# Where tiles lie in on-chip memory: a hybrid attention block with its working tiles placed anew

## The chip, the cores and the metric

The kernel runs on one core of a Trainium2 chip. The core has a matrix engine (TensorE, PE in the profile, with its weight load as PEld), a vector engine (VectorE, DVE), a scalar engine (ScalarE, ACT), GpSimd (POOL), and SyncE (SP), whose queue issues the DMAs. All of them work on one memory of 128 partitions; a tile takes the same stretch of bytes in each partition, so its address is an offset into the partition. The metric is the device time of one execution in microseconds; of several runs the median counts.

## The reference

One layer of a hybrid encoder on x of 1024 tokens by 1024 channels, float32:

```python
h = rms_norm(x, g_pre)
u = einsum('bsd,dn->bsn', h, w_in)            # 10 parts of 512 columns and 3 x 1024 merge gates
y_pool = pool_mixer(pool_v, pool_w, pool_scale) * silu(pool_g)
y_conv = conv_mixer(conv_x, conv_gb, conv_gc, conv_w, conv_b) * silu(conv_g)
y_sb   = stick_breaking_attention(sb_q, sb_k, sb_v) * silu(sb_g)
proj   = einsum('bsnw,nwd->bsnd', stack([y_pool, y_conv, y_sb], 2), w_branch)
merged = sum(sigmoid(merge) * proj, axis=2)
out    = einsum('bsd,de->bse', merged, w_out)
return x + rms_norm(out, g_post)
```

## The kernel before

Every float32 operand of a large product is split into a rounded high part and the remaining low part (`split`, L72: ACT casts the high part at L73, DVE or POOL subtracts at L74). A product of two operands then is three matmuls: high by high, high by low, low by high. TensorE works with a stationary operand of 128 columns and a moving operand of up to 512 columns; a `128x512` matmul is the unit in nearly all that follows. PE works off its instructions in the order of the program, and so does every other engine.

The stages, with their times in the profiled execution:

- **0 to 34 us**: x is normed and transposed into the tiles `hh` and `hl` (high and low part of h).
- **34 to 338 us**: attention, with the input projections that it needs in its gaps (`half_block`, L189), and then two products of the scheme below.
- **338 to 383 us**: the attention branch's projection (`branch_proj`, L491): 8 blocks of 24 matmuls, whose moving operands are the y tiles `yhi`, `ylo`. Beside it DVE and ACT form sums of quarters of h, `t1`, `t2`, `t3` (`build_quarters`, each with a high and a low tile); a fourth, t4, overwrites b12 in `hh`, `hl`.
- **383 to 919 us**: 24 pairs of input-projection blocks (4 for the pool branch, 8 for the conv branch, 12 for the merge gates). Each pair takes seven quarter products instead of eight (`run_pair`, L564; `product`, L530), each of 12 matmuls, in the order b11, t2, b21, t3, t1, t4, b22. So 36 of a pair's 84 matmuls read a `t1`, `t2` or `t3` tile, and 48 read `hh` and `hl`. The small matmuls `mx` of the pool branch (L648, 24 in all) and the projections of the pool and conv branches (L491) lie between pairs.
- **919 to 968 us**: the last four conv projections. For each half of a block, DVE multiplies the projection by the gate (L716), POOL adds the partial sum (L717), ACT casts the merged result's high part `m` and DVE subtracts its low part (L73, L74, called from `take_merged`, L732). In the same stretch the weights of the output projection are split (`oh`, `wo`).
- **968 to 1048 us**: the output projection (`out_products`, L791): its stationary operands are the `m` tiles, its moving ones `oh` and `wo`.

Weights come in by DMA (`w_raw`, `s_raw`), are cast by ACT and subtracted by POOL, two weights ahead of the product that reads them; three buffers each hold the high and the low parts (`wsp`). What fixes an address are the pools: they are stacked in the order in which they are opened, from the lower end upward, or with `side="right"` from the upper end downward. A pool with `reuse_waits="tile"` may take the place of tiles whose last use is still to come; its first write then waits for that use.

The merged result for channels 0 to 511 (d below 4) is finished early, kept in device memory (`proj_d`), and fetched again near the end, in `taken_back`:

```python
m = held["m"].tile([P, S], F32, tag="mr", name="mr", bufs=2)
nc.sync.dma_start(m, proj_d[d])
take_merged(d, slice(0, S), m)
```

The first of these steps is called ahead of the four last projections, and one more step with each half of a projection (`take`, L762). `mr` and the four `m` tiles lie in a pool `fin` that is opened where `t1`, `t2` and `t3` were.

## Time and profile before

| | us |
|---|---|
| median of 3 runs (1045.95 to 1049.87) | 1049.41 |
| the profiled execution | 1049.73 |
| its span, first to last instruction | 1048.0 |
| PE busy | 1004.6 (96%) |
| DVE, POOL, ACT busy | 625.9, 460.1, 449.4 |
| mean granted TensorE clock | 0.988 |

About 1.7 us of the profiled execution lie outside its span. PE is busy nearly throughout; consecutive matmuls overlap (the one begins while the other drains), so the cost of a matmul in a full stretch is the time from its start to the next one's start, which is less than the duration that the profile gives for one. The chain of waits that ended last shows it: a piece `x192` of 44.88 us holds 192 matmuls, one every 44.88 / 192 us.

### The profile page before, as it was taken

To read this page: it belongs to the slowest core of one execution; us is meant where nothing else is said; L and a number is where in the kernel's file an instruction comes from. 1 tells how busy PE (TensorE), PEld (TensorE's weight loads), DVE (VectorE), ACT (ScalarE), POOL (GpSimd) and SP (SyncE) were. 2 spreads that over 40 slices of the span, in tenths; PEclk is the share of its full clock that TensorE was granted. 3 is DMA by queue.
4 is the path that set the end of the run, shared out by engine and by line. 5 is a ranking of instruction groups with operands and counts; after the bars stand their busy time and mean duration, and the time that the engine had idled before them with its cause. 6 is when DMAs were issued, how large, how long until landed. Compare 5 with 4: busy or idle time off the path is not lost.

```text
span 1048.0 us, 13308 instructions
## 1 busy us (share of the span) xinstructions
PE 1004.6 (96%) x4752; PEld 829.0 (79%) x4752; DVE 625.9 (60%) x847; ACT 449.4 (43%) x879; POOL 460.1 (44%) x367
## 2 busy tenths in 40 slices
PE   4999999999998999999999999998999999998997
PEld 3788878888887888888888888886888888876886
DVE  6556777667777968798677675554333543342133
ACT  6567667567755543332222234333233332443111
POOL 3043544535472024455454444444555555576000
PEclk9999999999999999999999999998999999999999
DMA  6101000101011532122122134545333454164033
GB/s 229 53 21 41 22 21 21 41 21 32 21 31 41 191 131 71 61 70 91 61 81 61 61 111 144 190 136 173 118 120 124 161 171 131 34 221 157 1 121 121
DMA packets 45138, 97.09 MB, mean 93 GB/s; under 512 B 5392, under 2 KB 5648, under 8 KB 45072
## 3 DMA queue, kind: packets, MB, share of 16 engines
q1 hardware_dynamic: 44928, 95.71, 28.0%
q8 instruction: 38, 0.62, 0.2%
q10 hardware_dynamic: 144, 0.52, 0.1%
q14 instruction: 28, 0.23, 0.1%
HBM read 73.15 MB, written 23.07 MB: 92 GB/s over the span
## 4 chain that ended last, share of the span: by engine, by line
PE 82%; ACT 5%; DVE 4%; POOL 4%; issue 3%; DMA 2%; POOLq 0%; SPq 0%; DVEq 0%; ACTq 0%
PE g_ps L539 26%; PE q_ps L539 17%; PE g_ps L189 12%; PE pp L491 10%; PE o_ps L796 7%; PE o L418 3%; PE tp L404 2%; DVE sn L386 2%; PE z L382 1%; PE z L379 1%; ACT sn L383 1%; POOL sp L388 1%; POOL g L717 1%; DMA pr<-yp 1%; DMA xt<-in_x_dram 1%
## 5 line engine op out<-in xcount | busy, mean ns | idle before, releaser
L74 POOL TENSOR_TENSOR w_lo<-s,w_hi 128x512 fp32r<-128x512 f32 x95 | 130.7, 1376 | 173.8 <-ACT w_hi L73 171.2
L74 POOL TENSOR_TENSOR w_lo<-s_raw,w_hi 128x512 fp32r<-128x512 f32 x70 | 94.6, 1351 | 102.6 <-ACT w_hi L73 96.8
L388 POOL TENSOR_TENSOR sp<-sp,sn 128x127 f32<-128x127 f32 (+3 forms) x64 | 81.2, 1272 | 132.8 <-DVE sn L386 69.0
L386 DVE TENSOR_TENSOR_SCAN sn<-sn,zeros 128x128 f32<-128x128 f32 (+3 forms) x64 | 100.6, 1574 | 48.2 <-ACT sn L383 45.5
L73 ACT CAST w_hi<-s 128x512 fp32r<-128x512 f32 x96 | 59.6, 621 | 134.1 <-PE g_ps L539 65.7
L73 ACT CAST w_hi<-s_raw 128x512 fp32r<-128x512 f32 x70 | 43.5, 621 | 138.2 <-PE g_ps L539 53.8
L189 PE MATMUL g_ps<-hh,w_hi 128*128 128x512 f32 x240 | 99.4, 414 | 0.3 <-ACT hh L285 0.3
L189 PE MATMUL g_ps<-hl,w_hi 128*128 128x512 f32 x240 | 94.5, 394 | 0.3 <-DVE hl L286 0.3
L189 PE MATMUL g_ps<-hh,w_lo 128*128 128x512 f32 x240 | 94.5, 394 | 0.0
L74 POOL TENSOR_TENSOR w_lo<-w_raw,w_hi 128x512 fp32r<-128x512 f32 x44 | 68.2, 1550 | 56.3 <-ACT w_hi L73 56.3
L539 PE MATMUL g_ps<-hh,w_hi 128*128 128x512 f32 x236 | 92.6, 392 | 0.0
L539 PE MATMUL g_ps<-hh,w_lo 128*128 128x512 f32 x236 | 92.1, 390 | 0.0
L539 PE MATMUL g_ps<-hl,w_hi 128*128 128x512 f32 x236 | 91.8, 389 | 0.0
L491 PE MATMUL pp<-yhi,w_lo 128*128 128x512 f32 x192 | 77.1, 402 | 5.0 <-ACT yhi L73 2.6
L491 PE MATMUL pp<-ylo,w_hi 128*128 128x512 f32 x192 | 76.8, 401 | 0.9 <-DVE ylo L74 0.9
L491 PE MATMUL pp<-yhi,w_hi 128*128 128x512 f32 x192 | 76.4, 399 | 0.0
L383 ACT ACTIVATE sn<-z 128x384 f32<-128x384 f32 (+2 forms) x96 | 47.9, 499 | 29.7 <-PE z L382 20.3
L232 DVE TENSOR_TENSOR wl<-tp,wh 128x512 fp32r<-128x512 f32 (+2 forms) x96 | 50.4, 545 | 15.4 <-ACT wh L405 14.9
L539 PE MATMUL q_ps<-hh,w_hi 128*128 128x512 f32 x148 | 58.1, 392 | 0.0
L539 PE MATMUL q_ps<-hh,w_lo 128*128 128x512 f32 x148 | 57.8, 391 | 0.0
L539 PE MATMUL q_ps<-hl,w_hi 128*128 128x512 f32 x148 | 57.5, 389 | 0.0
L405 ACT CAST wh<-tp 128x512 fp32r<-128x512 f32 (+2 forms) x96 | 44.6, 493 | 21.8 <-PE tp L404 17.2
(204 smaller groups left out, 2426.4 us busy)
## 6 DMA issues: line engine op xcount, KB each, us to landing
s_raw<-in_w_in_dram SPq DMA_DIRECT2D x96, 256.0 KB, 2.6
pr<-proj SPq DMA_DIRECT2D x48, 256.0 KB, 3.3
proj<-g SPq DMA_DIRECT2D x20, 512.0 KB, 2.9
w_raw<-in_w_in_dram SPq DMA_DIRECT2D x34, 256.0 KB, 2.6
w_raw<-in_w_branch_dram SPq DMA_DIRECT2D x24, 256.0 KB, 2.6
xt<-in_x_dram SPq DMA_DIRECT2D x8, 512.0 KB, 7.9
proj<-proj SPq DMA_DIRECT2D x8, 512.0 KB, 2.7
wo_raw<-in_w_out_dram SPq DMA_DIRECT2D x16, 256.0 KB, 2.9
```

The source lines that it names most:

```text
L73: nc.scalar.copy(hi, raw)
L74: eng.tensor_tensor(out=lo, in0=raw, in1=f32(hi), op=ALU.subtract)
L189: nc.tensor.matmul(ps, l[:, a], r[k // 4][t][:, k % 4, :], start=(n == 0), stop=(n == 3 * KB - 1))
L232: nc.vector.tensor_tensor(out=o, in0=a, in1=f32(b), op=ALU.subtract)
L383: nc.scalar.activation(sn[:, c0:c1], z[:, :w], AF.Sigmoid, scale=-0.125)
L386: nc.vector.tensor_tensor_scan(out=rev, data0=rev, data1=zeros.to_broadcast([P, n]), initial=1.0, op0=ALU.mult, op1=ALU.max)
L388: nc.gpsimd.tensor_tensor(out=sp[:, 0:n - 1], in0=sp[:, 0:n - 1], in1=sn[:, 1:n], op=ALU.mult)
L405: nc.scalar.copy(wh[c][:, 0:m, qsub], tp[:, 0:m, :])
L418: nc.tensor.matmul(o[:, cs], vc[:, j, s, :], wt[j // 4][:, j % 4, cs], start=(j == 0 and wt is wl), stop=(j == i and wt is wh))
L491: nc.tensor.matmul(pp, l[:, a], r[:, HALVES[t]], start=(n == 0), stop=(n == 3 * NB - 1))
L539: nc.tensor.matmul(bank, l[:, a], r[:, j, :], start=(n == 0), stop=(n == 11))
L796: nc.tensor.matmul(ps, l[:, a], r[:, es], start=(d == 0 and n == 0), stop=(d == KB - 1 and n == 2))
```

## The change

The calculation and PE's order of instructions stay as they are. The pools `wraw`, `ysb`, `sraw`, `ssum`, `gates` and `tmps` move to the upper end; `quarters`, `stp` and `ysp` move to the lower side. The pool of the quarter sums is never closed: the `m` tiles of d below 4, a tile `back` in place of the two `mr`, and a tile `late` for the post-norm gain are further tiles of it.

```diff
-    wraw = op("wraw", 3)
+    wraw = op("wraw", 3, side="right")
-    ysb_pool = ysb_stack.enter_context(tc.tile_pool(name="ysb", bufs=4))
+    ysb_pool = ysb_stack.enter_context(tc.tile_pool(name="ysb", bufs=4, side="right"))
...
-    tpool, close_t = pool_of("quarters", 6, side="right")
+    tpool = op("quarters", 6, reuse_waits="tile")
...
-    stp, close_stp = pool_of("stp", 2, side="right")
-    ysp, close_ysp = pool_of("ysp", 4, side="right")
+    ysp, close_ysp = pool_of("ysp", 4)
+    stp, close_stp = pool_of("stp", 2)
...
-    held["raw"] = op("sraw", 5, reuse_waits="tile")
-    held["sum"] = op("ssum", 3, reuse_waits="tile")
+    held["raw"] = op("sraw", 5, side="right", reuse_waits="tile")
+    held["sum"] = op("ssum", 3, side="right", reuse_waits="tile")
...
-    tmps, close_tmps = pool_of("tmps", 1, side="right")
+    gpool = op("gates", 4, side="right", reuse_waits="tile")
+    tmps = op("tmps", 1, side="right", reuse_waits="tile")
...
-    gpool = op("gates", 4, reuse_waits="tile")
...
-            o = (held["m"].tile([P, 2, S], F32R, tag="m", name="m", bufs=4) if d < 4
-                 else bigp.tile([P, 2, S], F32R, tag="big", name="m"))
+            o = tpool.tile([P, 2, S], F32R, tag="t", name="m") if d < 4 else bigp.tile([P, 2, S], F32R, tag="big", name="m")
...
+        back = tpool.tile([P, 2, S], F32, tag="t", name="back")
...
-                m = held["m"].tile([P, S], F32, tag="mr", name="mr", bufs=2)
+                m = back[:, d % 2, :]
...
-    close_tmps()
-    close_t()
-    held["m"] = op("fin", 1, side="right", reuse_waits="tile")
...
-    fin = held["m"]
-    gpost_sb = fin.tile([P, D], F32, tag="gpost", name="gpost_sb")
+    fin = op("fin", 1, reuse_waits="tile")
+    late = tpool.tile([P, 2, S], F32, tag="t", name="late")
+    gpost_sb, junk = late[:, 0, :], late[:, 1, 0:HALF]
```

The addresses that follow from it, in KiB from the start of a partition, with the remainder of the start address by 64 bytes (all are multiples of 32):

| tiles | read by TensorE | before, KiB | rest | after, KiB | rest |
|---|---|---|---|---|---|
| `w_hi`, `w_lo` | yes | 24 to 36 | 0 | 18 to 30 | 0 |
| `hh`, `hl`; `m` of d from 4, `oh` | yes | 36 to 100 | 0 | 30 to 94 | 0 |
| `t1`, `t2`, `t3` | yes | 176 to 224 | 32 | 94 to 142 | 0 |
| y of the attention branch | yes | 124 to 156 | 32 | 142 to 174 | 0 |
| y of the pool and conv branches, `wo` | yes | 136 to 168 | 0 | 142 to 174 | 0 |
| `ph`, `pl` (read by `mx`) | yes | 124 to 132 | 0 | 190 to 198 | 32 |
| `m` of d below 4 | yes | 185 to 217 | 32 | 102 to 118, 126 to 142 | 0 |
| `mr`; after `back` | no | 177 to 185 | 32 | 118 to 126 | 0 |
| `w_raw`, `s_raw`, `s` | no | 18 to 24, 100 to 116 | 0 | 202 to 224 | 32 |
| gates, `pr` | no | 116 to 136 | 0 | 182 to 202 | 32 |
| `m1`, `u2`, `u3` | no | 170 to 176 | 32 | 176 to 182 | 32 |

All operands that TensorE reads in the attention stage start at a rest of 0 before and after.

The new places let some instructions be written earlier. On ACT, around the last pair of merge gates, the order before is this (`g_8288` and `g_8289` are the last pair's gates, `w_hi_...` its weights and the next projection's, `m_8439` and `m_8474` the high parts of d = 0 and 1):

```order
L73 CAST w_hi_8350<-s_raw_8242 128x512
L594 ACTIVATE g_8288<-g_8288 128x512
L73 CAST w_hi_8370<-s_8368 128x512
L73 CAST w_hi_8392<-w_raw_8390 128x512
L594 ACTIVATE g_8289<-g_8289 128x512
L73 CAST w_hi_8413<-w_raw_8411 128x512
L73 CAST m_8439<-mr_8437 128x1024
L594 ACTIVATE g_8289<-g_8289 128x512
L73 CAST m_8474<-mr_8472 128x1024
L73 CAST w_hi_8453<-w_raw_8451 128x512
L594 ACTIVATE g_8288<-g_8288 128x512
```

The same place of ACT after, where the `m` tiles of d = 0 to 3 are 8434, 8468, 8494 and 8530:

```order
L73 CAST w_hi_8350<-s_raw_8242 128x512
L73 CAST m_8434<-back_8432 128x1024
L595 ACTIVATE g_8288<-g_8288 128x512
L73 CAST w_hi_8370<-s_8368 128x512
L73 CAST m_8468<-back_8432 128x1024
L73 CAST w_hi_8392<-w_raw_8390 128x512
L73 CAST m_8494<-back_8432 128x1024
L595 ACTIVATE g_8289<-g_8289 128x512
L73 CAST w_hi_8413<-w_raw_8411 128x512
L73 CAST m_8530<-back_8432 128x1024
L595 ACTIVATE g_8289<-g_8289 128x512
```

All four casts now stand among the last pair's weight casts; before, two stood behind them and the other two among the projections. The first `back` transfer waits for the last product that reads `t2` (its place in memory); the transfers into the same half of `back` (d = 2 after 0, 3 after 1) wait for DVE's subtraction of the earlier one.

On DVE before, from the last pair into the last projections (`g_8136` and `g_8137` are gates of the pair before, `pp` a projection's result, `m_8496` and `m_8560` the merged blocks of d = 4 and 5):

```order
L585 TENSOR_TENSOR g_8289<-g_ps_8396,u3_8292 128x512
L74 TENSOR_TENSOR m_8439<-mr_8437,m_8439 128x1024
L585 TENSOR_TENSOR g_8288<-g_ps_8417,u2_8291 128x512
L74 TENSOR_TENSOR m_8474<-mr_8472,m_8474 128x1024
L716 TENSOR_TENSOR g_8136<-pp_8457,g_8136 128x512
L74 TENSOR_TENSOR m_8496<-g_8136,m_8496 128x512
L716 TENSOR_TENSOR g_8136<-pp_8481,g_8136 128x512
L74 TENSOR_TENSOR m_8501<-mr_8499,m_8501 128x1024
L74 TENSOR_TENSOR m_8538<-mr_8536,m_8538 128x1024
L716 TENSOR_TENSOR g_8137<-pp_8519,g_8137 128x512
```

The same stretch of DVE after (there `m_8490` and `m_8552` are the blocks of d = 4 and 5):

```order
L74 TENSOR_TENSOR m_8434<-back_8432,m_8434 128x1024
L586 TENSOR_TENSOR u3_8292<-q_ps_8354,u2_8291 128x512
L74 TENSOR_TENSOR m_8468<-back_8432,m_8468 128x1024
L586 TENSOR_TENSOR u2_8291<-g_ps_8374,u2_8291 128x512
L586 TENSOR_TENSOR g_8289<-g_ps_8374,u3_8292 128x512
L74 TENSOR_TENSOR m_8494<-back_8432,m_8494 128x1024
L586 TENSOR_TENSOR g_8289<-g_ps_8396,u3_8292 128x512
L74 TENSOR_TENSOR m_8530<-back_8432,m_8530 128x1024
L586 TENSOR_TENSOR g_8288<-g_ps_8417,u2_8291 128x512
L715 TENSOR_TENSOR g_8136<-pp_8452,g_8136 128x512
L74 TENSOR_TENSOR m_8490<-g_8136,m_8490 128x512
L715 TENSOR_TENSOR g_8136<-pp_8475,g_8136 128x512
```

The subtractions for d = 2 and 3, which stood between two multiplications of the last projections, now stand among the last pair's sums. At the start of the pool branch (383 us) a few casts and memsets change places as well.

## Rows read from the trace of the kernel before

**Rows 1.** Stretches: start:end, length, busy (count) by engine, PEclk, DMA share, GB/s.
```profile
338.00:383.00 45.00, 45.00 (x195) 35.94 (x194) 38.40 (x61) 22.71 (x41) 1.29 (x1) 1.00 0.49 169
701.00:720.00 19.00, 15.50 (x61) 11.24 (x60) 10.12 (x14) 8.94 (x16) 6.61 (x5) 0.90 0.47 150
912.00:968.00 56.00, 48.94 (x205) 39.16 (x204) 20.46 (x29) 23.06 (x39) 38.85 (x28) 0.95 0.57 188
```

**Rows 2.** Chain that ended last: start us, us, what, count.
```profile
337.79 44.88 PE pp L491 x192
...
749.06 10.88 PE pp L491 x48
...
967.66 73.90 PE o_ps L796 x334
```

**Rows 3.** Stretch of five pairs, line L539 alone: PE and PEld busy (count), clock, DMA.
```profile
562.47:659.27 96.80, 96.80 (x421) 78.81 (x421) 1.00 0.33 108
```

**Rows 4.** PE's groups by shape, whole span: out<-in, count, busy us, mean ns.
```profile
L539 PE MATMUL g_ps<-hh,w_hi 128*128 128x512 f32 x236 | 92.6, 392 | 0.0
...
L539 PE MATMUL g_ps<-hl,w_hi 128*128 128x512 f32 x236 | 91.8, 389 | 0.0
...
L796 PE MATMUL o_ps<-wo,m 128*128 128x512 f32 x168 | 38.8, 392 | 0.0
...
L539 PE MATMUL g_ps<-t2h,w_hi 128*128 128x512 f32 x60 | 23.8, 396 | 0.0
...
L648 PE MATMUL mx<-ph,pwl 128*128 128x512 f32 x8 | 3.1, 389 | 0.0
```

**Rows 5.** PE's groups by shape from 338 to 382.6 us.
```profile
L491 PE MATMUL pp<-ylo,w_hi 128*128 128x512 f32 x64 | 25.2, 396 | 0.0
```

**Rows 6.** PE's groups by shape from 749.1 to 759.9 us.
```profile
L491 PE MATMUL pp<-ylo,w_hi 128*128 128x512 f32 x16 | 6.2, 389 | 0.0
```

**Rows 7.** DVE's instructions, 916 to 970 us: start, us, out<-in, [idle before <-releaser].
```profile
922.40 0.69 DVE L716 TENSOR_TENSOR g<-pp,g 128x512 f32<-128x512 f32 x1 [0.81 <-PE pp L491]
...
927.13 1.22 DVE L74 TENSOR_TENSOR m<-mr,m 128x1024 fp32r<-128x1024 f32 x1
930.14 1.69 DVE L74 TENSOR_TENSOR m<-mr,m 128x1024 fp32r<-128x1024 f32 x1 [1.80 <-ACT m L73]
...
942.20 0.68 DVE L716 TENSOR_TENSOR g<-pp,g 128x512 f32<-128x512 f32 x1
...
945.54 0.68 DVE L716 TENSOR_TENSOR g<-pp,g 128x512 f32<-128x512 f32 x1
...
950.59 0.68 DVE L716 TENSOR_TENSOR g<-pp,g 128x512 f32<-128x512 f32 x1
...
953.94 0.68 DVE L716 TENSOR_TENSOR g<-pp,g 128x512 f32<-128x512 f32 x1
```

**Rows 8.** PE's waits: what waited, for what: us in total, times, longest.
```profile
PE o_ps L796 <- DVE o L817: 4.7, 1, 4.7
```

**Rows 9.** ACT's instructions, 916 to 970 us.
```profile
964.92 1.32 ACT L73 CAST wo<-wo_raw 128x512 fp32r<-128x512 f32 x2 [1.29 <-DMA wo_raw<-in_w_out_dram]
966.14 0.59 ACT L808 ACTIVATE junk<-o_ps 128x512 f32<-128x512 f32 x1
```

**Rows 10.** The tile `mr`: casts (duration ns min/median/max, starts), time to landing.
```profile
L73 ACT CAST m<-mr x4: 1037/1048/1052, 917.3 to 929.1; 128x1024 fp32r<-128x1024 f32 x4
...
DMA to landing us min/median/max: 3.1/4.7/5.9
```

**Rows 11.** ACT's groups by shape, the cast of `ph`.
```profile
L73 ACT CAST ph<-pb 128x1024 fp32r<-128x1024 f32 x4 | 4.2, 1052 | 8.4 <-DVE pb L670 4.5 <-DVE pb L658 3.9
```

**Rows 12.** The page's costliest groups: mean ns, then idle time before them.
```profile
L74 POOL TENSOR_TENSOR w_lo<-s,w_hi 128x512 fp32r<-128x512 f32 x95 | 130.7, 1376 | 173.8 <-ACT w_hi L73 171.2
...
L73 ACT CAST w_hi<-s 128x512 fp32r<-128x512 f32 x96 | 59.6, 621 | 134.1 <-PE g_ps L539 65.7
```

## The prediction

> **What bounds the kernel now.** I read the stretches first: from 338 to 383 us PE is busy for all of its 45.00 us at a granted clock of 1.00, and the only long stretches where it is not are the one around 710 us and the one from 912 us on [rows 1]. So outside those two the time is the number of PE's matmuls times the distance from one to the next. The chain of waits then gives that distance, since a piece of it holds a known count: the attention branch's projection takes 44.88 us for 192 matmuls, 233.75 ns each; a later projection of the same shape takes 10.88 us for 48, 226.67 ns each [rows 2]. [...] The groups by shape repeat it in the durations: 396 ns in the first stage [rows 5], 389 ns in the second [rows 6]. Over the whole span it is 396 for a matmul that reads `t2`, 389 for one that reads `hl`, and 389 for `mx` [rows 4].

> Beside the table of addresses this sorts cleanly. Whatever has 396 has an operand that starts at a rest of 32 bytes by 64; whatever has 389 has only rests of 0. Height does not sort it: the slow y tiles lie at 124 to 156 KiB, the fast ones at 136 to 168, the fast `ph` at 124. Two rows lie between, 392 ns for `hh` with `w_hi` (389 for `hl` with `w_hi`, the same addresses) and 392 for the output projection [rows 4]. The first I read as an after-effect: the matmul that begins a product behind a `t` product still pays. The second is a mean of m tiles of both rests.

> **The change part by part.** The sum is made against the profiled execution, 1049.73 us (span 1048.0 and 1.7 around it), which stands 0.3 us above the median.

> 1. Attention branch's projection. All 192 matmuls come to rest 0: 44.88 less 192 x 226.67 ns = 43.52 gives **1.36 us**, on the path, since PE is never idle there [rows 1, 2].

> 2. The 24 pairs. Five pairs, from 562.47 to 659.27, take 96.80 us for 5 x 84 = 420 matmuls (the row's count of 421 includes one at the edge) [rows 3]. At 226.67 ns they are 95.20; so 1.60 per five, 0.32 per pair, 7.68 for 24. That holds the 36 slow matmuls (36 x 7.1 ns = 0.26) and the after-effect behind them (0.06). Before 720 us PE waits for work that DMAs bring, 15.50 us busy of 19.00 [rows 1]; what PE gains shortly ahead of it, I take about half a pair's worth, 0.2, is lost again there. **7.5 us**.

> 3. Output projection. The 168 matmuls of `wo` have a mean of 392 against 389: 168 x 3 ns = 0.50. The 192 of `oh` read the same m tiles; 334 matmuls lie in the last piece [rows 2], 168 of them 512 columns of `wo` and 48 narrow ones, which leaves 118 of `oh`: 118 x 3 = 0.36. **0.86 us**.

> 4. The other way round: `ph`, `pl` come to a rest of 32, and their 24 matmuls pay 7.1 ns, 0.17, and about as much behind them. **-0.33 us** at most.

> 5. The end of the gates, 912 to 968 us. PE is busy for 48.94 of 56 us there [rows 1], and its longest wait, 4.7 us, is for DVE's scaling of the first output [rows 8]: that waits for ACT's `junk`, which runs at 966.14 right behind the last casts of `wo`, whose DMAs have just landed [rows 9]. What paces this stretch is a round over DVE, POOL, ACT and DVE: the multiplications by the gate start at 922.40 and, seven rounds later, at 953.94, 31.54 us [rows 7]. Rounds without an `mr` subtraction take 3.34 us (942.20 to 945.54) or 5.05 (945.54 to 950.59), in turn, as POOL has no `oh` subtraction in between or two. Seven rounds at that pace, four short and three long, are 28.5; with the last one as measured, about 28.65. So up to **2.9 us** could come from moving the two subtractions at 927.13 and 930.14 (1.22 and 1.69 us) and their casts (1.05 each) ahead of the projections, where the order of DVE now has them among the last pair's sums. The lower end is 0: the first two casts of `mr` leave the stretch as well, but the chain of `wo` transfers behind it may have its own pace. I take 2.2, three quarters, being nearer to the clean rounds, which are rows of this very stretch.

> What I cost at nothing: raw weights, gates and partial sums at a rest of 32 for ACT, DVE and POOL. ACT's cast from and to tiles at 32 takes 1048 ns [rows 10], the same shape at 0 takes 1052 [rows 11]. POOL at 32 is in no row; were it 3% slower, as PE is, its 1376 ns would grow by 41 ns, and 173.8 us of idle time before 95 of them hide that [rows 12]. In the seven rounds of part 5 it would be 0.3 us on the path, which I keep for the range; a gain there is as large at most. The attention stage has rests of 0 in both, so nothing. The moves at 383 us put one cast of `pwh` ahead of two weights; PE waits for no weight there.

> Sum: 1.36 + 7.5 + 0.86 - 0.33 = 9.4 from reads, 2.2 from the end, 11.6. 1049.73 - 11.6 = 1038.1; I say **1038.0**.

> [...]

> **The rivals.**

> *Reads gain, the end does not.* The stretch from 919 us is set by the `wo` transfers and their casts [rows 9] rather than by the rounds, or the late `back` takes the place of the late `mr`. For it: ACT's last `wo` casts end right at the wait's end, and a DMA ended the idle time before them. Against it: these transfers can only start when the projections have read the y tiles that `wo` overlays, so they come earlier with the rounds. 1049.73 - 9.4 = **1040.3 us**.

> *Addresses do not matter to PE.* Something else makes the `t` matmuls slow, such as POOL's and DMAs' traffic, or the sums of different weights. Against: slow and fast products alternate within each pair under the same traffic. Only part 5 stays: 1049.73 - 2.2 = **1047.5 us**.

> *Half of it.* The after-effect has another cause and stays, or rests of 32 in the tiles that DVE, ACT and DMAs use slow PE too: 4.7 from reads, 1.0 from the end, **1044.0 us**.

> *Slower: `back` comes too late.* In the new order of ACT the cast from `back` stands ahead of `w_hi_8370`, the weight of the last pair's b22, and ACT works in order. Behind a late transfer PE would stop. From the end of the last t2 product, which frees `back`, to the start of b22 lie four products of 12: 10.88 us. The weight itself can only be cast from the end of t3 on, 5.44 us after t2's end, and cast and subtraction (0.62 + 1.38 [rows 12]) leave 3.44 us of its own 5.44. Less the 1.05 of the m cast and some 0.62 for the gate's activation between them (as long as a cast of its shape), `back` may land 5.44 + 3.44 - 1.67 = 7.2 us after its issue without any cost. `mr` took 3.1 to 5.9 [rows 10]. Two landings stand in series (d = 2 waits for d = 0), so at x us each the cost is 2 (x - 7.2): at 13 us it eats the 11.6, and at 14 us the time is 1049.73 - 9.4 - 2.2 + 13.6 = **1051.7 us**. Four transfers of 512 KB issued close together speak for longer landings; that the longest seen is 5.9 speaks against.

> **How the numbers follow.** The forecast 0.60, no gain at the end 0.23, addresses without effect 0.07, half of it 0.07, slower 0.03. The range for 8 in 10 reaches up to the second and over it, to 1043.5, short of the half case; down to 1033: 0.7 more from the end, and the 3.5 us by which the fastest run of before lies under its median. About 0.5%, 5 us, is what a measurement tells from no change: below 1044.2 is faster, above 1054.7 slower. Forecast, second case and most of the half case count as faster, 0.89; the address case and the rest as same, 0.08; slower 0.03.

> **What would show it.** `t` rows at 389 to 390 ns instead of 395 or 396; the attention branch's 192 matmuls in about 43.5 us; five pairs in 95.2; `hh` with `w_hi` and the output projection at 389; `mx` at 395. Gate multiplications of the last projections 28.5 to 29.5 us from first to last. POOL's and ACT's means within 1%, and the wait around 710 us still there. It is wrong if the `t` rows stay at 395 (addresses do not matter), if they fall and the stretch at 919 us keeps its length (second case), or if PE shows a wait for `w_hi` at about 905 to 920 us (slower).

## The result and the profile after

The changed kernel takes 1037.78 us (median of 4 runs, 1035.81 to 1039.87) against 1048.99 (4 runs, 1045.95 to 1049.87): a ratio of 0.9888, interval 0.9866 to 0.9909. The forecast was 1038.0. The profiled execution has a span of 1038.1 us, 9.9 less than before.

The chain of waits after, for the pieces that answer to [rows 2] (start, us, what, count):

```profile
338.17 43.62 PE pp L491 x192
...
742.59 10.88 PE pp L491 x48
...
958.64 73.05 PE o_ps L793 x334
```

The first piece lost 1.26 us, the last 0.85; the later projection kept its 10.88. The five pairs that answer to [rows 3], in the view by stretches (PE, PEld, DVE, ACT and POOL busy, clock, DMA share, GB/s):

```profile
546.37:641.57 95.20, 95.20 (x421) 78.83 (x421) 67.28 (x79) 29.66 (x50) 47.76 (x35) 1.00 0.29 95
```

96.80 became 95.20, 226.67 ns a matmul. PE's groups by shape say the same, against [rows 4]:

```profile
L539 PE MATMUL g_ps<-hh,w_hi 128*128 128x512 f32 x236 | 91.9, 389 | 0.0
...
L793 PE MATMUL o_ps<-wo,m 128*128 128x512 f32 x168 | 38.2, 389 | 0.0
...
L539 PE MATMUL g_ps<-t2h,w_hi 128*128 128x512 f32 x60 | 23.3, 389 | 0.0
...
L649 PE MATMUL mx<-ph,pwl 128*128 128x512 f32 x8 | 3.2, 398 | 0.0
```

`t2` fell from 396 to 389 and took the `hh` rows behind it from 392 along; `mx` alone rose. PE's waits:

```profile
PE o_ps L793 <- DVE o L813: 5.5, 1, 5.5
...
PE q_ps L539 <- POOL w_lo L74: 0.8, 1, 0.8
```

The first is the wait of [rows 8], 0.8 us longer; the second is new. The end of the gates, DVE's multiplications against [rows 7] and POOL's first instructions in that stretch (start, us, what, idle before):

```profile
914.12 0.69 DVE L715 TENSOR_TENSOR g<-pp,g 128x512 f32<-128x512 f32 x1 [0.46 <-PE pp L491]
...
918.72 0.68 DVE L715 TENSOR_TENSOR g<-pp,g 128x512 f32<-128x512 f32 x1
...
924.21 0.68 DVE L715 TENSOR_TENSOR g<-pp,g 128x512 f32<-128x512 f32 x1
...
927.55 0.68 DVE L715 TENSOR_TENSOR g<-pp,g 128x512 f32<-128x512 f32 x1
...
944.33 0.68 DVE L715 TENSOR_TENSOR g<-pp,g 128x512 f32<-128x512 f32 x1
```

```profile
913.63 1.30 POOL L74 TENSOR_TENSOR oh<-wo_raw,oh 128x512 fp32r<-128x512 f32 x1 [2.15 <-ACT oh L73]
914.90 1.28 POOL L74 TENSOR_TENSOR w_lo<-w_raw,w_hi 128x512 fp32r<-128x512 f32 x1
916.15 1.28 POOL L716 TENSOR_TENSOR g<-pr,g 128x512 f32<-128x512 f32 x1
```

Seven rounds take 30.21 us, not 31.54, and not the 28.65 of the clean pace: the first multiplication ends at 914.81, but POOL is in an `oh` and then in a `w_lo` subtraction, and adds at 916.15.

Set end to end, before less after: start to 338 us -0.38; the attention branch's projection 1.26; from its end to the first gate multiplication 539.73 - 532.33 = 7.40; from there to PE's restart 45.26 - 44.52 = 0.74; the output projection 0.85. Together 9.87, the 9.9 of the spans. The -0.38 comes from the clock. From 321.6 to 325.0 us, in the attention stage, the granted clock was 0.51 after and 1.00 before; just ahead of it PE was busy for 1.68 of 3.60 us after and for 1.67 before. After, then before (length, PE busy and count, clock, DMA share, GB/s):

```profile
321.60:325.00 3.40, 3.40 (x13) 0.51 0.00 0
321.60:325.00 3.40, 2.79 (x17) 1.00 0.00 0
```

PE had been 0.4 us ahead and lost 0.8 there. The first experiment below has the same spell at 322.1 us with the old order, the second does not have it with the new one (mean granted clock from 34 to 332 us 0.99 and 1.00), so no run ties it to the change.

### The profile page after: what moved, and what is told of

Same layout as the page of the kernel before. It is cut to its first block, busy times and chain, and to the rows that moved or that the text cites. A ratio compares the mean times of both kernels' runs of the same rounds, so it can differ in the third digit from the quotient of the medians.

```text
span 1038.1 us, 13307 instructions
## 1 busy us (share of the span) xinstructions
PE 996.2 (96%) x4752; PEld 829.4 (80%) x4752; DVE 623.1 (60%) x847; ACT 449.5 (43%) x879; POOL 458.6 (44%) x367
## 3 DMA queue, kind: packets, MB, share of 16 engines
q1 hardware_dynamic: 44928, 95.71, 28.6%
## 4 chain that ended last, share of the span: by engine, by line
PE 81%; ACT 5%; DVE 4%; POOL 4%; issue 3%; DMA 2%; SPq 0%; POOLq 0%; DVEq 0%; ACTq 0%
PE g_ps L539 25%; PE q_ps L539 17%; PE g_ps L189 12%; PE pp L491 10%; PE o_ps L793 7%; PE o L418 3%; PE tp L404 2%; DVE sn L386 2%; PE z L382 1%; PE z L379 1%; DMA wo_raw<-in_w_out_dram 1%; ACT sn L383 1%; POOL sp L388 1%; POOL g L716 1%; POOL w_lo L74 1%
## 5 line engine op out<-in xcount | busy, mean ns | idle before, releaser
L73 ACT CAST w_hi<-s_raw 128x512 fp32r<-128x512 f32 x70 | 43.5, 622 | 134.2 <-PE g_ps L539 53.6
L539 PE MATMUL g_ps<-hh,w_hi 128*128 128x512 f32 x236 | 91.9, 389 | 0.0
L539 PE MATMUL g_ps<-hl,w_hi 128*128 128x512 f32 x236 | 91.8, 389 | 0.0
L539 PE MATMUL g_ps<-hh,w_lo 128*128 128x512 f32 x236 | 91.8, 389 | 0.0
L539 PE MATMUL q_ps<-hh,w_lo 128*128 128x512 f32 x148 | 57.7, 390 | 0.8 <-POOL w_lo L74 0.8
L539 PE MATMUL q_ps<-hh,w_hi 128*128 128x512 f32 x148 | 57.6, 389 | 0.0
L539 PE MATMUL q_ps<-hl,w_hi 128*128 128x512 f32 x148 | 57.6, 389 | 0.0
```

What stands on the lines that cost most here:

```text
L73: nc.scalar.copy(hi, raw)
L539: nc.tensor.matmul(bank, l[:, a], r[:, j, :], start=(n == 0), stop=(n == 11))
```

## The experiments

Theory A is the prediction's: an operand at a rest of 32 bytes by 64 costs PE some 7 ns per matmul. Rival H: the height of the tile. Rival N: neither, something else in the change.

**The kernel before, with nothing but the last bits of addresses changed.** It gets 32 unused bytes at the upper end:

```diff
+    padr = op("padr", 1, side="right")
+    padr.tile([P, 8], F32, name="pad_r")
```

> The kernel before with 32 unused bytes per partition at the upper end: every tile of the upper side starts 32 bytes lower, at a rest of 0 by 64; no tile moves up or down by more, and the order of instructions stays. If the rest of the address by 64 bytes sets PE's pace: t rows at 389 ns, the attention branch's 192 matmuls in 43.5 us, 9.4 to 9.7 us less than before (ratio 0.991), and the last projections as long as before (31.5 us for seven rounds). If the height in memory sets it: t rows stay at 395 to 396 and the time is that of before (ratio 1.000). If something else in the change did it: no change either.

Measured: 1040.7 us against 1049.03, ratio 0.9918 (0.9900 to 0.9936). The `t` tiles lie at 176 to 224 KiB as before, and cost 389 ns:

```profile
L541 PE MATMUL g_ps<-t2h,w_hi 128*128 128x512 f32 x60 | 23.3, 389 | 0.0
...
L650 PE MATMUL mx<-ph,pwl 128*128 128x512 f32 x8 | 3.1, 389 | 0.0
```

The attention branch's projection took 43.70 us, the seven rounds 31.59. So 32 bytes do most of what the change does, and height alone makes no `t` row slow. H and N fall. The gain is 8.3 us, where 9.4 to 9.7 were expected; 0.9 us goes to a wait for w_lo that is told in the next section.

**The changed kernel, with the same pad.** The diff is the same, on the changed kernel.

> The changed kernel with the same 32 bytes at the upper end: gates, partial sums, raw weights and ph, pl come to a rest of 0, TensorE's low tiles stay. Address rest and PE alone: the mx matmuls fall from 395 to 389 ns, 0.2 to 0.3 us less than the changed kernel, which is no difference in time (1037.5, ratio to before 0.989). If DVE, ACT or POOL also pay for a rest of 32: their means for gates, casts of raw weights and subtractions fall by 1 to 3%, and the time by up to 1 us more. If height made mx slow: 395 ns stay.

Measured: 1037.83 us, ratio 0.9886 (0.9864 to 0.9907), the changed kernel's within both intervals. `mx` is back at 389. ACT's activation of the gates, POOL's addition of partial sums and DVE's gate multiplication have 631, 1290 and 689 ns, against 632, 1290 and 689 at a rest of 32: these instructions show no cost of a rest of 32.

**All low tiles 32 bytes up.** The test that A should have won:

```diff
+    pad_l = const.tile([P, 8], F32, name="pad_l")
```

> The changed kernel with its lower side shifted up by 32 bytes: heights stay to within 32 bytes, but every operand that TensorE reads (weights, hh, hl, t, y, m, oh, wo) starts at a rest of 32. Address rest: some 3,700 matmuls of 512 columns pay 7.1 ns, +26 us, 1064 us, if moving and stationary operand together cost no more than one of them; if they add, 6 ns more each, +48 us, 1086. Height: 1038 as the changed kernel.

Measured: 1040.11 us (2 runs), ratio 0.9910 (0.9881 to 0.9939). Every operand of the rows below and of the other large products starts at a rest of 32 (only small constants stay at 0), and nothing is slow:

```profile
L540 PE MATMUL g_ps<-hh,w_hi 128*128 128x512 f32 x236 | 91.9, 389 | 0.0
...
L540 PE MATMUL g_ps<-t2h,w_hi 128*128 128x512 f32 x60 | 23.3, 389 | 0.0
```

A falls as it was put: a rest of 32 is not slow by itself (226.8 ns from start to start).

**Only the weights 32 bytes up.** All moving operands stay at 0:

```diff
+    op("pad0", 1).tile([P, 8], F32, name="pad_0")
     wsp = op("wsp", 3)
+    op("pad1", 1).tile([P, 8], F32, name="pad_1")
```

> The changed kernel with only the weights w_hi, w_lo (stationary operands of some 3,300 matmuls of 512 columns) at a rest of 32, and all moving operands at 0. If a stationary operand at 32 costs what m seems to cost in the output projection before (about 6 ns): +20 us, 1058 us, hh rows at 395. If a weight load beside a matmul hides it: 1038 and 389 ns, and only the moving operand counts.

Measured: 1053.97 us (8 runs), ratio to before 1.0046 (1.0031 to 1.0061), 16 us above the changed kernel. Now `hh`, at a rest of 0 as ever, is slow, and `m` with `wo`, both at 0, is not:

```profile
L541 PE MATMUL g_ps<-hh,w_hi 128*128 128x512 f32 x236 | 93.3, 395 | 0.0
...
L795 PE MATMUL o_ps<-wo,m 128*128 128x512 f32 x168 | 38.2, 389 | 0.0
...
L541 PE MATMUL g_ps<-t2h,w_hi 128*128 128x512 f32 x60 | 23.7, 395 | 0.0
```

With the run before it this gives theory B: what counts is the distance between the addresses of a moving operand and of the weights, not where either lies. In the kernel before the weights were at 0, so that a rest of 32 and a distance of 32 were the same thing.

**Other distances.** t1, t2, t3 moved within tiles that are 64 bytes longer:

```diff
+    rest = {"t1": 4, "t2": 8, "t3": 1}
...
+    def slot(name, at=0, dt=F32R):
+        return tpool.tile([P, 4 * HALF + 16], dt, tag="t", name=name)[:, at:at + 4 * HALF]
...
```

> The changed kernel with the quarter tiles moved off the place of the weights by other amounts. Distance of the moving tile's address from the stationary one's, by 128 bytes: t1h 16, t1l 80, t2h 32, t2l 96, t3h 4, t3l 68; hh and hl stay at 0. (The t tiles in the kernel before: 32, and 233.5 ns from one matmul to the next; the all-shifted run: 0 everywhere, and 226.8, which refuted the rest of each address by itself.) If every distance that is no multiple of 64 costs one more unit read: all six at 233.5 ns, durations 395, time 1045. If the cost grows with the distance: about 230 at 16, 227.6 at 4, 233.5 at 32, time 1041. If the rest of the moving tile alone counted, all the same as the first, but the run with shifted weights and moving tiles at 0 speaks against it.

Measured: 1052.12 us (one run). Neither: the time lies above both. The y tiles, not meant to be touched, moved by 384 bytes with the longer tiles, and their matmuls went from 226.7 ns to some 232.7, though their distance is still a multiple of 64 and of 128. The row of one of their shapes has 394 ns in the changed kernel and 400 here:

```profile
L491 PE MATMUL pp<-ylo,w_hi 128*128 128x512 f32 x192 | 76.7, 400 | 1.1 <-DVE ylo L74 1.1
```

So the run says that 64 is not the period, and its `t` rows mix too many distances to say more.

**Distances of 64, 128 and 192, all else at 256.** The same slots without `rest`, and 128 bytes behind them to bring y back to a multiple of 256:

> The changed kernel with t tiles at other multiples of 64 bytes from the weights, all else at multiples of 256: t1h and t2h at 0, t1l at 64, t2l at 192, t3h at 128, t3l at 64. If only the place within 64 bytes counts: all rows at 226.8, 1038 us. If the distance counts by 256 bytes (y at 128 had 232.7 where it had been 226.7 at 0 and at 256; m at 64 had 229.0): t3h about 232 to 233, t1l and t3l about 229, t2l 229 to 233, t1h and t2h 226.8; 1040 us.

Measured: 1045.47 us (one run), `t` rows at 390 to 397 ns:

```profile
L544 PE MATMUL g_ps<-t3h,w_hi 128*128 128x512 f32 x56 | 22.3, 397 | 0.0
L544 PE MATMUL g_ps<-t1h,w_hi 128*128 128x512 f32 x56 | 22.2, 396 | 0.0
L544 PE MATMUL g_ps<-t1l,w_hi 128*128 128x512 f32 x56 | 22.1, 395 | 0.0
```

The place within 64 bytes is refuted as the law; but t1h, at a distance of 0, is as slow as its neighbours at 64, and the expected amounts fail. The three matmuls of a t1 product, of which one lies at 64 and two at 0, take 700 ns from start to start, 20 more than at 0 throughout. So in this run a slow matmul drags the next ones.

**Which weights a matmul pays for.** A first run moved only w_lo:

```diff
-        lo = wsp.tile([P, HALF], F32R, tag="lo", name="w_lo")
+        lo = wsp.tile([P, HALF + 32], F32R, tag="lo", name="w_lo")[:, 8:8 + HALF]
```

> The changed kernel with only w_lo (every third stationary operand) 32 bytes off all other operands. Which of two neighbours counts: if a matmul pays for the distance between its own two operands, the rows hh with w_lo go to 233.5 ns from their start to the next (5.5 us over the some 780 products' matmuls, plus the projections), the rows hl with w_hi, behind which w_lo is loaded, stay at 226.8. If it pays for its moving operand against the weights loaded beside it for the next, it is the rows hl with w_hi. If both, or a longer memory, all three rise. Time about 1044 to 1050.

It took 1051.71 us (one run), but the longer tiles had moved all others by 384 bytes against w_hi, which by the runs above is slow in itself; it tells nothing. The second has tiles 256 bytes longer (`HALF + 64`), so that only w_lo is off:

> The changed kernel with only w_lo 32 bytes off and every other distance a multiple of 256 bytes (in the run before this one with w_lo off, all other tiles had moved by 384 bytes against w_hi, so it told nothing). If a matmul pays for the distance between its own two operands: hh with w_lo at 233.5 ns, the two others at 226.8; sum of three matmuls 687. If its moving operand is held against the weights loaded beside it for the next matmul: hl with w_hi at 233.5, the others 226.8. If neither alone, all three between. Time about 1045.

Measured: 1053.12 us (one run).

```profile
L539 PE MATMUL g_ps<-hl,w_hi 128*128 128x512 f32 x236 | 94.3, 400 | 0.0
L539 PE MATMUL g_ps<-hh,w_hi 128*128 128x512 f32 x236 | 93.2, 395 | 0.0
L539 PE MATMUL g_ps<-hh,w_lo 128*128 128x512 f32 x236 | 91.8, 389 | 0.0
```

The matmul that uses w_lo does not pay: 389 ns, 228.2 to the next start. The one before it pays most: 400 ns, 239.0. It is the one beside which w_lo is loaded (PE and PEld: start, us, what):

```profile
519.98 0.40 PE L539 MATMUL q_ps<-hl,w_hi 128*128 128x512 f32 x1
519.99 0.19 PEld L539 LDWEIGHTS q_ps<-hh,w_lo 128*128 128x128 f32 x1
520.22 0.39 PE L539 MATMUL q_ps<-hh,w_lo 128*128 128x512 f32 x1
```

The one behind it pays too: 395 ns, 232.7. Three together take 700 ns, where 680 would be free, as much as three with all weights off (233.33 each). So one stray operand in three is as dear as three, and the time is 1053 us, not the 1045 expected. A price that each matmul pays at once for the distance to its own weights does not give this, by durations or by starts; one on the weights that are loaded beside it does, if the delay also reaches a matmul further on. This is a fit and no proof: a disturbed pace took five to seven matmuls to settle (next section), so a price of the matmul with w_lo itself, which shows only in those behind it, is not excluded.

**The end of the gates: POOL's w_lo.** On the changed kernel with the pad, DVE subtracts the last four projections' w_lo:

```diff
-                yield loaded(w_branch[n], nc.gpsimd)
+                yield loaded(w_branch[n], nc.vector if n >= KB + 4 else nc.gpsimd)
```

> The changed kernel with the 32-byte pad at the upper end, and the low parts of the last four projections' weights subtracted by DVE, not POOL. Theory on the end of the gates: the two w_lo subtractions on POOL in the first two rounds (1.25 us ahead of an addition, 0.43 beside a subtraction of DVE) are why seven rounds take 30.2 to 30.7 us and not the 28.65 that the clean rounds gave. Then the rounds become 3.35 and 5.05 from the first on, 28.6 in all, 1.7 us less. Rival: the late oh transfer ahead of the first round sets it; then the first round stays above 4.2.

Measured: 1037.85 us (one run), against 1037.83 with the pad alone, so the time does not show the gain. In its profiled execution the first round is 3.34 us in place of 4.69, the second still 5.50, and seven rounds are 28.96 in place of 30.36 with POOL's subtractions.

```profile
913.65 0.68 DVE L717 TENSOR_TENSOR g<-pp,g 128x512 f32<-128x512 f32 x1
...
916.99 0.68 DVE L717 TENSOR_TENSOR g<-pp,g 128x512 f32<-128x512 f32 x1
...
922.49 0.68 DVE L717 TENSOR_TENSOR g<-pp,g 128x512 f32<-128x512 f32 x1
```

The w_lo that stood ahead of the first addition explains 1.4 of the missing 1.7 us, and the rival, the late `oh`, falls. The rest, in the second round, is not explained by it.

**A faster round.** With the pad, DVE adds the partial sum in the last four projections:

```diff
+            eng = nc.gpsimd if take is None else nc.vector
-            nc.gpsimd.tensor_tensor(...)
+            eng.tensor_tensor(...)
```

> The changed kernel with the 32-byte pad, and in the last four projections DVE adds the partial sum in place of POOL. If the round over DVE, POOL, ACT, DVE paces the end of the gates and the wo chain follows it: a round is then 0.68 + 0.68 + 0.62 + 0.69 and some gaps, 2.8 to 3.0 us, and PE (2.72 us for a half) nearly the bound; seven rounds 20 to 21 us in place of 30.2, the restart of PE 5 to 9 us earlier, 1029 to 1033. If the chain of wo transfers has its own pace: rounds shorter, but the restart no earlier, 1037.

Measured: 1031.09 us (4 runs), ratio 0.9831 (0.9792 to 0.9869). The first and the last multiplication and the first scaling (DVE: start, us, what, idle before):

```profile
914.96 0.69 DVE L717 TENSOR_TENSOR g<-pp,g 128x512 f32<-128x512 f32 x1 [0.49 <-PE pp L493]
...
940.76 0.68 DVE L717 TENSOR_TENSOR g<-pp,g 128x512 f32<-128x512 f32 x1
...
952.81 0.68 DVE L816 TENSOR_TENSOR o<-o_ps,late 128x512 f32<-128x512 f32 x1
```

Seven rounds take 25.80 us, not 20 to 21: DVE's additions take 0.7 to 1.7 us and twice wait for `pr` to land. The restart follows: the first scaling comes 37.9 us after the first multiplication, against 43.4 with the pad alone. So the rounds do pace the end.

**And the transfers of wo ahead.** In addition eight raw buffers for the second half of the output weights, and DVE for every second subtraction:

```diff
+        wo[1].append(out_weight(..., d, HALVES[1],
+                                wraw if d < 3 else held["raw"], nc.vector if d % 2 else nc.gpsimd))
```

> The kernel with the 32-byte pad and DVE's additions, and for the second half of the output weights eight raw buffers in place of three (five of the pool of the raw pair weights), every second low part subtracted by DVE. If the wo transfers, three at a time, and POOL's eight subtractions set the restart of PE (12.05 us from the last gate multiplication to the first scaling in the run with DVE's additions, PE waiting 2.8 us): that stretch falls to some 8 us, PE's wait goes, 1027 to 1029 us. If the transfers are slow because eight come at once, or the freeing of the y tiles' place is what they wait for: the stretch stays at 11 to 12, 1031.

Measured: 1030.87 us (5 runs), ratio 0.9819 (0.9805 to 0.9834). The same instructions of DVE here:

```profile
917.62 0.67 DVE L717 TENSOR_TENSOR g<-pp,g 128x512 f32<-128x512 f32 x1
...
942.38 0.68 DVE L717 TENSOR_TENSOR g<-pp,g 128x512 f32<-128x512 f32 x1
...
952.05 0.68 DVE L817 TENSOR_TENSOR o<-o_ps,late 128x512 f32<-128x512 f32 x1
```

The last stretch falls from 12.05 to 9.67 us, not to 8, and PE's wait for the scaling is gone from the list. But the first multiplication comes 2.7 us later, behind a subtraction from `back` on DVE (915.33, 1.76 us), so that the first scaling is only 0.8 us earlier. The time is the same as the run before within both intervals: the gain of 2 us is not shown. This kernel is faster than the changed one, whose interval begins at 0.9866; its median is the lowest of those run.

## Why the prediction was right, and where not

*Part 1, attention branch's projection.* 1.36 us forecast, 1.26 found. Right.

*Part 2, the pairs.* 7.5 us forecast, 7.40 found, and 1.60 per five pairs to the hundredth. But the 7.40 is a sum of more than the forecast named. The pool branch has a new wait, 0.8 us, for w_lo at 470 us. ACT and POOL there, after (start, us, what, idle before):

```profile
467.98 1.05 ACT L73 CAST ph<-pb 128x1024 fp32r<-128x1024 f32 x1 [5.26 <-DVE pb L671]
```

```profile
469.63 1.98 POOL L74 TENSOR_TENSOR w_lo<-s_raw,w_hi 128x512 fp32r<-128x512 f32 x1 [4.13 <-ACT w_hi L73]
```

ACT's weight cast stands behind the cast of `ph`, which waits for DVE; PE now comes early enough to feel it. The wait is there in the padded kernel before as well (0.9 us), whose order and layout are otherwise the old ones, and not in the list of the run with slow weights, so that the faster PE is the likely cause and the new places are not. The forecast had no wait for weights here. Against it, the part of the chain around 710 us that holds no PE, but transfers and splits, shrank from 16.44 to 15.00 us, where the forecast had it lose 0.2. That is scatter of the execution as far as the runs show: from the start of the last pair matmul ahead of it (711.44 us before) to the matmul with which PE goes on (719.99) it is 8.56 us before, 7.24 after, but 8.88 in the changed kernel with the pad. Without the wait and this gain the part would be some 6.8, so 7.40 fits partly by luck.

*Part 3, output projection.* 0.86 forecast, 0.85 found. *Part 4, `mx`.* Right in sign: 389 ns before, 393 to 398 after, by group.

*The reading behind parts 1 to 4* was right for this change and wrong as a rule. The 7.1 ns a matmul of parts 2 and 4 are 233.75 less 226.67, and the granted clock was 1.00 in both pieces (the second from 749.06 to 759.94 us). "Whatever has 396 has an operand that starts at a rest of 32" held in the kernel before because the weights lay at 0 throughout. The run with everything at 32 and the one with only the weights at 32 turn it round. The `392` of `hh` was read rightly as an after-effect of a `t` product, but it is not one matmul that pays: the starts in the product behind `t1` or `t2` lie 240, 225, 231, 236, 229, 232 and 231 ns apart and then 227 (means of 46 products), 36 ns in all. Behind a wait the pace settles like this at a distance of 0 too: after the one for w_lo at 470 us, 336, 236, 229, 232, 231 and then 227.

With the other engines' instructions unchanged, PE's pace was 226.8 ns at a distance of 0 and 233.3 at 32 (only the weights moved). What the runs separate is PE's matmul and PE's own weights.

*Part 5, the end of the gates.* This is the step that failed in size: 2.2 us forecast, 0.74 found. The rounds gave 1.33. By its rows the clean pace is 28.5 us (the last round measures 3.35), not the 28.65 it used. The clean rounds were taken from the end of the stretch, where POOL has no w_lo left; the first rounds have one ahead of an addition, which the forecast left out beside `mr`. The other 0.6 went between the last multiplication and the restart: 13.58 us to the first scaling after, 12.99 before. The first scaling after, then before:

```profile
957.91 0.68 DVE L813 TENSOR_TENSOR o<-o_ps,late 128x512 f32<-128x512 f32 x1
966.93 0.68 DVE L817 TENSOR_TENSOR o<-o_ps,gpost_sb 128x512 f32<-128x512 f32 x1
```

In other runs of the changed order this stretch is 13.01 us (with the pad), 12.90 (all low tiles shifted) and 13.75 (weights shifted), so no run ties the 0.6 to the change. That the landing of the `wo` transfers sets it is likely, but not shown.

*The rivals.* `back` landed in 3.2 to 5.9 us, and no PE wait for the last pair's weights is in the list: not late. The case without any gain at the end (1040.3) is about what the padded kernel before shows, 1040.7. That the forecast fits the median to 0.2 us is partly luck: the sum was 11.6 against the profiled execution, where the profiled pair gives 9.9 and the medians 11.2.

## What to carry to other kernels

Where PE is busy throughout, divide a piece of the chain by its count and compare the same shape across stages: 7 ns in 227 are found in no list of waits. Before moving tiles to other pools, look at the distances between moving operands and weights; here 32 unused bytes alone brought the ratio to 0.9918, and the whole change to 0.9888. And take a clean round's pace from the rounds that will be left, with all that their slowest engine still holds.
